# One Gram block moved into the first Gram group on two projection banks, three groups shifted, and some weights at another offset in their slots

## The chip, the core and the metric

The kernel runs on one core of a Trainium2 chip. A core has a matrix engine (TensorE; PE in the profile, PEld for its weight loads), a vector engine (VectorE, DVE), an activation engine (ScalarE, ACT), a general engine (GpSimd, POOL) and a queue that issues transfers (SyncE, SP). Each engine works through its own list in order and waits on semaphores of the others. Matrix products are written into PSUM, which has eight banks of 512 float32 values in each of 128 partitions; the other engines read them from there. The metric is device microseconds of one launch, a median over runs.

## What is computed

One layer of a hybrid trunk on 528 tokens (16 meta tokens and 512 inputs) of width 2048: an RMS norm, one input projection, an RWKV-7 branch of 16 heads of 64, a gated short convolution, one output projection, and a last RMS norm. Cut to what matters here:

```python
P = rmsnorm(h_res) @ w_in                     # columns: r, k, v, g of 1024 each, 128 low-rank, 4 x 1024 for the convolution
Pr = Pr + (prev - Pr) * mu_shift              # token shift
decay = exp(-exp(w_raw)); a = sigmoid(a0 + al @ a_lora_up)
kk = k * k_k / norm(k * k_k)                  # per head
for each token:                               # per head, state S of 64 x 64
    S = S * decay - (S @ kk) (kk * a)^T + v k^T
    y = S @ r
y_a = (groupnorm(y) + bonus) * silu(g_r)
y_b = Bg * conv3(Cg * hc) * silu(g_c)
out = rmsnorm(h_res + concat(y_a, y_b) @ w_out)[16:]
```

The recurrence is done in nine chunks: chunk 0 holds the meta tokens, chunks 1 to 8 hold 64 tokens each. For each pair of heads (0 to 7 in the code) and each chunk, products between the decayed keys, removal vectors and queries of the chunk are needed: the Gram blocks.

## The kernel before

**Projection.** 65 column tiles of 128 are projected one after another. Operands are split into a high and a low part (`xh`, `xl` for the normalised input, `hi`, `lo` for the weights), and a product is three matmuls: hi with xh, hi with xl, lo with xh (`steps`). A tile of type k, v or low-rank takes all 528 tokens in two ranges of 256 and 272 columns; r, g, C and h take ranges of 256 and 258; B and gc take one range of 512. A tile (`main`) walks through four quarters of the contraction, in each first one range and then the other. For k the second range comes first. Each range has a PSUM bank from the pool `pm` (four banks, tag "main"), so that two tiles of two ranges fit: while one is computed, the other is read out (`scaled`, the rows named `pr_...`, `u`, `hh`, `b`, `gc` in the profile).

**Weights.** A quarter tile of weights arrives in a `raw` buffer (rows `wr`), ACT casts it to `hi`, and DVE or POOL makes `lo` (rows `w`, lines 134 and 135). Six slots of 1152 values hold them. `column` says at which value in its slot a tile's weights begin: 0, 16 or 80. In the built program the slots and the rows of `xh` and `xl` begin at the same place modulo 512 bytes, so these three columns are distances of 0, 64 and 320 bytes (320 is 192 below 512) between the weights and the input that is multiplied with them.

**Order of the work.** PE's list is written by the program itself. `fill(ns)` emits projection steps, counted at 0.43 ns for each column, until the given time is used up; between two fills the smaller work of the recurrence is emitted. The lists of DVE, ACT, POOL and SP come from a scheduler, in which `ahead()` gives some instructions a priority. Some transfers are queued by `later(ns, ...)` on the same count. Transfers of weights and of intermediate results stand in one list on SP.

**Around the change.** `prepare(i)` makes one head pair's operands: two low-rank products (`tz`, `ta`, lines 571 and 572), the tiles `bk` and `ar`, and the split squares `sq` and products `rk`. Then, before the change: a fill; a first Gram group for chunks 0 to 7 (line 681, 32 matmul records of 64 rows by 128 columns, into two banks of the pool `pz`, tag "tz", and two of `pi`, tags "misc" and "ser"); four masked copies to `gt` (line 691); a fill of 5500; a second group with chunk 8's two products, into two new "tz" tiles, one of which holds half of the norms `n2` as well; the norms (lines 713 and 714) and the bonus sums `zb`; and two more masked copies. After that `gt` goes to memory and back for a triangular solve (rows `nd`, `y`, `prod`, `tt` on DVE). The tiles `hh` and `cv` belong to the convolution.

Later stages, a recurrence over chunks (from 631 us on, among the last projection tiles) and the output projection (line 1243), are not touched.

Of the kernel before, what the change touches and what calls it, by code (L numbers as in the profile page):

```python
# [9 lines left out]
F32 = mybir.dt.float32  # L10
# [8 lines left out]
P = 128  # L19
# [6 lines left out]
NCH = SEQ // CH + 1  # L26
LP = NCH * CH
# [15 lines left out]
FW = dict(  # L43
    evac=34, start=1062, lora=2200, gram=8000, gram_b=13500, gram2=5500, misc=2000, v=2000, vt=1000, solve=24500, solve_first=30000,
    tr=3200, lev=3000, cp=4200, out=1500, begin=19500, p=2900, u=2900, s=5200, last=3700, mix=2600,
)
# [31 lines left out]
def hymba_kernel(ctx: ExitStack, tc: tile.TileContext, xt, xtok, front, w_in, w_out, pv, lup, cst, msk, gf, out):  # L78
# [35 lines left out]

    def column(j):
        what = plan[j][0]
        return {"B": 0, "gc": 0, "v": 80, "g": 80, "h": 80}.get(what, 16)
    stream += [w_out[0, g] for g in range(3)]
    quarters, chain, low = {}, {}, {}
    state = {"next": 0}  # L120
# [17 lines left out]
    def prefetch(upto):  # L138
        while state["next"] < min(upto, len(stream) if chain else N_IN):
            j = state["next"]  # L140
            raw = chain[j - N_IN] if j >= N_IN else wp.tile([P, 1024], F32, tag="raw", name=f"wr{j}", bufs=3)
            state["dma"] = nc.sync.dma_start(raw, stream[j]).ins
            with tc.high_priority(offset=WEIGHTS):
                for q in range(2):
                    split_w(2 * j + q, raw[:, q * 512 : (q + 1) * 512], nc.gpsimd if q and 10 < j < N_IN else nc.vector)
            state["next"] = j + 1
# [19 lines left out]
    pm = ph1.enter_context(tc.tile_pool(name="pm", bufs=4, space=PSUM))  # L166
    pz = ph1.enter_context(tc.tile_pool(name="pz", bufs=2, space=PSUM))
    pi = ph1.enter_context(tc.tile_pool(name="pi", bufs=1, space=PSUM))
# [150 lines left out]
    def steps(ps, ranges, k4, q, ks=range(4), rs_=range(2)):  # L319
        hi, lo = quarters[q]  # L320
        for r, (a, b) in enumerate(ranges):
            if r not in rs_:
                continue
            for k in ks:
                kt = 4 * k4 + k
                w = slice(k * P, (k + 1) * P)
                for n, (ww, xx) in enumerate(((hi, xh), (hi, xl), (lo, xh))):
                    nc.tensor.matmul(  # L328
                        ps[r], ww[:, w], xx[:, kt, a:b], start=(kt == 0 and n == 0), stop=(kt == KT - 1 and n == 2)
                    )  # L330
                    yield (b - a) * 0.43

    def banks(ranges, name, pool, tag):
        return [pool.tile([P, b - a], F32, tag=tag, name=f"ps_{name}_{r}") for r, (a, b) in enumerate(ranges)]

    def main(j, ranges, name):
        prefetch(2 * j + 4)
        ps = banks(ranges, name, pm, "main")
        for k4 in range(4):
            if k4 == 1:  # L340
                prefetch(2 * j + 5)
            for r in (1, 0) if name[0] == "k" else range(len(ranges)):
                yield from steps(ps, ranges, k4, 4 * j + k4, rs_=(r,))
        return ps

# [196 lines left out]
    def step():  # L542
        t = next(flow, None)
        if t is None:
            run_pending(float("inf"))
        else:
            clock[0] += t
            run_pending(clock[0])
        return t

    def fill(ns):
        while ns > 0:
            seen = len(ready)
            t = step()
            if t is None:
                return
            ns -= t
            if len(ready) > seen:
                ns += FW["evac"]
# [5 lines left out]
    def low_rank(i, j, up, w0, name, pad):  # L565
        t = tr(name)
        nc.gpsimd.memset(t[:, META:CH], pad)
        hi, lo = up
        for a, b in ((0, 272), (272, L)):
            z = pz.tile([P, b - a], F32, tag="tz", name=f"{name}_{a}")  # L570
            nc.tensor.matmul(z, hi[:, j], la[:, j, a:b], start=True, stop=False)
            nc.tensor.matmul(z, lo[:, j], la[:, j, a:b], start=False, stop=True)
            with tc.high_priority(offset=AHEAD):
                if a == 0:
                    nc.scalar.activation(t[:, 0:META], z[:, 0:META], AF.Tanh, bias=w0, scale=0.5)
                    nc.scalar.activation(t[:, CH : 5 * CH], z[:, META:272], AF.Tanh, bias=w0, scale=0.5)
                else:
                    nc.scalar.activation(t[:, 5 * CH : LP], z, AF.Tanh, bias=w0, scale=0.5)
            fill(FW["lora"])
        return t  # L580
# [46 lines left out]
    def prepare(i):  # L627
        p = i % 2
        until("k", i)
        k = got["k", i]  # L630
# [6 lines left out]
        tz = low_rank(i, 0, up, hv[:, 0, i : i + 1], f"tz{i}", -1.0)  # L637
# [26 lines left out]
        r = got["r", i]  # L664
# [8 lines left out]
        nc.scalar.activation(sq, k, AF.Square, scale=col(V_KK, i))  # L673
        sqh, sql = split(sq, f"sq{i}", LP)
        rh, rl = split(r, f"rk{i}", SEQ)
        fill(FW["gram_b" if p else "gram"])

        gt = cq.tile([P, 2, NCH, P], F32, tag=f"gt{p}", name=f"gt{i}")
        def gram(z, c, c0):
            for h, hs, ho in heads:  # L680
                nc.tensor.matmul(
                    z[h][:, c - c0],
                    bk[hs, c, h : h + 2, :].rearrange("p a s -> p (a s)"),
                    ar[hs, c].rearrange("p a s -> p (a s)"),
                    start=True, stop=True,
                )

        def masked(z, c0, c1):
            with ahead():
                for h in range(2):  # L690
                    nc.vector.tensor_tensor(
                        out=gt[:, h, c0:c1],
                        in0=z[h],
                        in1=gmask[:, h].unsqueeze(1).to_broadcast([P, c1 - c0, P]),
                        op=ALU.mult,
                    )


        za = [pz.tile([P, 4, P], F32, tag="tz", name=f"g{i}_0_{h}") for h in range(2)]
        zc = [pi.tile([P, 4, P], F32, tag=("misc", "ser")[h], name=f"g{i}_4_{h}") for h in range(2)]  # L700
        for c in range(8):
            gram(za if c < 4 else zc, c, c // 4 * 4)
        masked(za, 0, 4)
        masked(zc, 4, 8)
        fill(FW["gram2"])

        ze = [pz.tile([P, P + 288 * (1 - h)], F32, tag="tz", name=f"g{i}_8_{h}") for h in range(2)]
        gram([z[:, 0:P].unsqueeze(1) for z in ze], 8, 8)
        n2 = tr(f"n2{i}")
        zn = pi.tile([2, 288], F32, tag="misc", name=f"n2_{i}")  # L710
        zs = ((zn, 0, 288), (ze[0][0:2, P : P + 288], 288, LP))
        for z, a, b in zs:
            nc.tensor.matmul(z, ones[:, P : P + 2], sqh[:, a:b], start=True, stop=False)
            nc.tensor.matmul(z, ones[:, P : P + 2], sql[:, a:b], start=False, stop=True)
# [3 lines left out]
        with ahead():  # L718
            for z, a, b in zs:
                nc.scalar.copy(n2[0:2, a:b], z)  # L720
            masked([z[:, 0:P].unsqueeze(1) for z in ze], 8, 9)
        nc.scalar.copy(r, zb)
        fill(FW["misc"])

# [90 lines left out]
        v = got["v", i]  # L815
# [547 lines left out]
    z = {}  # L1363
    for u, unit in enumerate(units):
        half, prod, g = unit
# [53 lines left out]
    with tc.manual_schedule(engines={mybir.EngineType.DVE, mybir.EngineType.Activation, mybir.EngineType.Pool}):  # L1419
# [16 lines left out]
        for part in range(2):  # L1436
# [7 lines left out]
            h = here(1, 2)[:, cols]  # L1444
# [73 lines left out]
```

## Time and profile before

| | |
|---|---|
| median of 3 runs | 1010.39 us (1008.97 to 1011.24) |
| the profiled execution | 1008.48 us |
| its span, first to last instruction | 1006.6 us |
| PE busy | 993.2 us (99%) |
| DVE / ACT / POOL busy | 683.2 / 393.0 / 288.0 us |
| granted TensorE clock, mean | 0.997 |
| first projection matmul to the last one | 4.6 to 842 us |

The span leaves 1.9 us of the profiled execution outside, and that execution is 1.9 us below the median. In the rows of the order of time, the first number is the start in microseconds from the span's start, the second the duration; matmul records overlap, so the pace of PE is the distance between two starts and not the duration. An idle time in square brackets names what ended it. In rows of waits, "<-" names who was waited for.

### The profile page before, as it was taken

Reading aid. Unit: us, or ns where it says so; the run is one execution under the profiler, and the core shown is the slowest. Engines: PE = TensorE matmul, PEld = TensorE weight load, DVE = VectorE, ACT = ScalarE, POOL = GpSimd, SP = SyncE. Lnnn points to the kernel's source line nnn. Section 1 sums busy time; section 2 is a strip of 40 time slices with the busy share of each in tenths; the row PEclk is TensorE's granted clock in tenths of the full one; section 3 lists DMA queues with packets and bytes.
Section 4 is the critical chain, followed back from the end, with each engine's and each line's share of the span. In section 5 each row is a group of like instructions: output and inputs, shape, how many; then the busy total and the mean of one; then the engine's idle time right before and its main releaser. Section 6 shows DMA issues by size and latency. Waiting matters only on the chain.

```text
span 1006.6 us, 23759 instructions
## 1 busy us (share of the span) xinstructions
PE 993.2 (99%) x9723; PEld 912.7 (91%) x9723; DVE 683.2 (68%) x1305; ACT 393.0 (39%) x729; POOL 288.0 (29%) x294
## 2 busy tenths in 40 slices
PE   9999999999999999999999999999999999999996
PEld 8999998999998999998999998889888898888775
DVE  7686955587765668654668654244555697999787
ACT  7553423344313434322434322222222336546453
POOL 0123313224223423232323222223332333047001
PEclk9999999999999999999999999999999999999998
DMA  9526476446674363854273856977673688796754
GB/s 338 155 70 154 115 205 159 125 125 146 155 186 146 94 171 99 218 152 119 85 175 94 222 141 192 340 237 234 216 216 95 177 271 235 210 281 146 173 130 168
DMA packets 185181, 175.35 MB, mean 174 GB/s; under 512 B 121584, under 2 KB 142832, under 8 KB 184560
## 3 DMA queue, kind: packets, MB, share of 16 engines
q1 hardware_dynamic: 182480, 164.92, 56.9%
q0 software_dynamic: 2304, 8.39, 4.9%
q8 instruction: 76, 1.25, 0.5%
q10 hardware_dynamic: 288, 0.52, 0.1%
q14 instruction: 33, 0.27, 0.1%
HBM read 137.44 MB, written 36.35 MB: 173 GB/s over the span
## 4 chain that ended last, share of the span: by engine, by line
PE 62%; DVE 5%; DMA 2%; issue 2%; ACT 0%; POOL 0%; DVEq 0%; ACTq 0%; POOLq 0%
PE ps_gc L328 8%; PE ps_B L328 7%; PE ps_h L328 7%; PE ps_C L328 7%; PE ps_k L328 5%; PE ps_v L328 5%; PE M L1243 5%; PE ps_g L328 5%; PE ps_r L328 5%; DVE o L1216 2%; PE P L1243 2%; DMA wo<-in_w_out_dram 2%; PE Q L1243 1%; PE zy L1010 1%; PE zs L1006 1%
## 5 line engine op out<-in xcount | busy, mean ns | idle before, releaser
L135 POOL TENSOR_TENSOR w<-wr,w 128x512 fp32r<-128x512 f32 x119 | 166.8, 1403 | 365.8 <-ACT w L134 317.5
L134 ACT CAST w<-wr 128x512 fp32r<-128x512 f32 x252 | 152.9, 618 | 280.9 <-PE ps_k L328 45.2
L135 DVE TENSOR_TENSOR w<-wr,w 128x512 fp32r<-128x512 f32 x133 | 95.9, 728 | 103.6 <-ACT w L134 93.3
L328 PE MATMUL ps_k<-xh,w 128*128 128x256 f32 (+1 forms) x512 | 95.7, 284 | 0.1
L328 PE MATMUL ps_r<-xh,w 128*128 128x256 f32 (+1 forms) x512 | 95.1, 281 | 0.0
L328 PE MATMUL ps_v<-xh,w 128*128 128x272 f32 (+1 forms) x512 | 95.0, 283 | 0.0
L328 PE MATMUL ps_h<-xh,w 128*128 128x258 f32 (+1 forms) x512 | 94.0, 282 | 0.0
L328 PE MATMUL ps_C<-xh,w 128*128 128x258 f32 (+1 forms) x512 | 93.2, 281 | 0.0
L328 PE MATMUL ps_g<-xh,w 128*128 128x258 f32 (+1 forms) x512 | 91.9, 281 | 0.0
L328 PE MATMUL ps_B<-xh,w 128*128 128x512 f32 x256 | 83.4, 395 | 0.1
L328 PE MATMUL ps_gc<-xh,w 128*128 128x512 f32 x256 | 81.7, 393 | 0.3 <-DVE w L135 0.3
L328 PEld LDWEIGHTS ps_h<-xh,w 128*128 128x128 f32 x512 | 79.7, 189 | 2.3 <-issue 1.6
L328 PEld LDWEIGHTS ps_k<-xh,w 128*128 128x128 f32 x512 | 80.3, 189 | 0.7 <-DVE w L135 0.3
L328 PEld LDWEIGHTS ps_r<-xh,w 128*128 128x128 f32 x512 | 80.3, 189 | 0.2
L328 PEld LDWEIGHTS ps_v<-xh,w 128*128 128x128 f32 x512 | 80.0, 189 | 0.3
L328 PEld LDWEIGHTS ps_C<-xh,w 128*128 128x128 f32 x512 | 79.6, 189 | 0.6
L328 PEld LDWEIGHTS ps_g<-xh,w 128*128 128x128 f32 x512 | 79.3, 189 | 0.4
L328 PE MATMUL ps_k<-xl,w 128*128 128x272 f32 (+1 forms) x256 | 72.9, 285 | 0.0
L328 PE MATMUL ps_v<-xl,w 128*128 128x256 f32 (+1 forms) x256 | 72.5, 283 | 0.0
L328 PE MATMUL ps_r<-xl,w 128*128 128x256 f32 (+1 forms) x256 | 72.4, 283 | 0.0
L328 PE MATMUL ps_g<-xl,w 128*128 128x256 f32 (+1 forms) x256 | 72.3, 282 | 0.0
L328 PE MATMUL ps_C<-xl,w 128*128 128x256 f32 (+1 forms) x256 | 71.9, 281 | 0.0
(320 smaller groups left out, 2288.2 us busy)
## 6 DMA issues: line engine op xcount, KB each, us to landing
wr<-in_w_in_dram SPq DMA_DIRECT2D x126, 512.0 KB
ct<-opd SPq DMA_DIRECT2D x64, 288.0 KB
wo<-in_w_out_dram SPq DMA_DIRECT2D x25, 512.0 KB
x<-in_w_out_dram POOLq DMA_DIRECT2D x16, 512.0 KB, 5.7
opd<-ar SPq DMA_DIRECT2D x8, 576.0 KB
opd<-gt SPq DMA_DIRECT2D x16, 288.0 KB
opd<-bt SPq DMA_DIRECT2D x64, 64.0 KB
x<-in_w_out_dram SPq DMA_DIRECT2D x8, 512.0 KB
```

Source lines behind the costliest of these rows:

```text
L134: nc.scalar.copy(hi, rq)
L135: low[q] = eng.tensor_tensor(out=lo, in0=rq, in1=hi.bitcast(F32), op=ALU.subtract).ins
L328: nc.tensor.matmul(ps[r], ww[:, w], xx[:, kt, a:b], start=(kt == 0 and n == 0), stop=(kt == KT - 1 and n == 2))
L1006: nc.tensor.matmul(d[hs, j], w, x[hs], start=(a == 0), stop=(a == b - 1))
L1010: nc.tensor.matmul(d[ho, j], t[hs, o : o + CH], x[hs], start=(a == 0), stop=(a == b - 1))
L1216: nc.vector.tensor_tensor(out=lo, in0=rq, in1=hi.bitcast(F32), op=ALU.subtract)
L1243: nc.tensor.matmul(bank[s], left(prod, jj, m, s), w, start=(jj == 0 and n == 0), stop=(jj == 7 and n == 2))
```

## The change

Four things are changed. Chunk 8's two products are emitted right after those of chunks 0 to 7, as part of the first Gram group, and go to two banks of the projection's pool `pm`; their masked copies follow the four others. The second half of the norms gets a tile of its own under the tag "tz". The first Gram group of pairs 0, 1 and 3 is moved by +2000, +2500 and -4000 of the fill's count, and the fill behind it gives that back, so that norms and bonus stay at their places. The weights of the low-rank tile and of k and r begin at column 80 of their slots (as those of v, g and h did), those of C stay at 16, B and gc at 0; and k walks through its ranges in the order of the others.

```diff
     def column(j):
         what = plan[j][0]
-        return {"B": 0, "gc": 0, "v": 80, "g": 80, "h": 80}.get(what, 16)
+        return {"B": 0, "gc": 0, "C": 16}.get(what, 80)
...
-            for r in (1, 0) if name[0] == "k" else range(len(ranges)):
+            for r in range(len(ranges)):
...
-        fill(FW["gram_b" if p else "gram"])
+        shift = {0: 2000, 1: 2500, 3: -4000}.get(i, 0)
+        fill(FW["gram_b" if p else "gram"] + shift)
...
-        for c in range(8):
-            gram(za if c < 4 else zc, c, c // 4 * 4)
+        ze = [pm.tile([P, 1, P], F32, tag="main", name=f"g{i}_8_{h}") for h in range(2)]
+        for c in range(NCH):
+            gram((za, zc, ze)[c // 4], c, c // 4 * 4)
         masked(za, 0, 4)
         masked(zc, 4, 8)
-        fill(FW["gram2"])
-
-        ze = [pz.tile([P, P + 288 * (1 - h)], F32, tag="tz", name=f"g{i}_8_{h}") for h in range(2)]
-        gram([z[:, 0:P].unsqueeze(1) for z in ze], 8, 8)
+        masked(ze, 8, 9)
+        fill(FW["gram2"] - shift)
+
         n2 = tr(f"n2{i}")
-        zn = pi.tile([2, 288], F32, tag="misc", name=f"n2_{i}")
-        zs = ((zn, 0, 288), (ze[0][0:2, P : P + 288], 288, LP))
+        zn = [pool.tile([2, 288], F32, tag=t, name=f"n2_{i}_{t}") for pool, t in ((pi, "misc"), (pz, "tz"))]
+        zs = ((zn[0], 0, 288), (zn[1], 288, LP))
...
-            masked([z[:, 0:P].unsqueeze(1) for z in ze], 8, 9)
```

On PE the two groups of pair 2 stand as follows before the change (`g2_4`, `g2_8`: Gram products of chunks 4 to 7 and of chunk 8; `ps_k3`, `ps_r3`: projection tiles; `n2_2`: norms). First the end of the first group, then, some 40 rows on, the second group:

```order
L681 MATMUL g2_4_0_2908<-ar2_2643,bk2_2644 128x128
L681 MATMUL g2_4_1_2909<-ar2_2643,bk2_2644 128x128
L328 MATMUL ps_k3_0_2827<-xh_110,w66_2632 128x256 x2
...
L328 MATMUL ps_r3_1_2979<-xh_110,w68_2682 128x258 x2
L681 MATMUL g2_8_0_3002<-ar2_2643,bk2_2644 128x128
L681 MATMUL g2_8_1_3003<-ar2_2643,bk2_2644 128x128
L713 MATMUL n2_2_3007<-sq2_h_2796,ones_114 2x288
```

And after it:

```order
L682 MATMUL g2_4_0_2910<-ar2_2645,bk2_2646 128x128
L682 MATMUL g2_4_1_2911<-ar2_2645,bk2_2646 128x128
L682 MATMUL g2_8_0_2912<-ar2_2645,bk2_2646 128x128
L682 MATMUL g2_8_1_2913<-ar2_2645,bk2_2646 128x128
L328 MATMUL ps_k3_1_2830<-xh_110,w66_2634 128x272 x2
...
L328 MATMUL ps_r3_1_2987<-xh_110,w68_2684 128x258 x2
L714 MATMUL n2_2_misc_3011<-sq2_h_2798,ones_114 2x288
```

Chunk 8's products now share the first group's entry and exit, and the second group begins with the norms. The banks that `g2_8` takes were those of tile v2, and the next tile, r3, takes them next.

On DVE around pair 3's Gram group, before the change (`pr_v3`: read-out of tile v3; `prod2`, `tt2`, `y2`: the solve of pair 2; `gt3`: masked copies):

```order
L352 TENSOR_TENSOR pr_v3_3355<-ps_v3_0_3190,rs_112 128x256
L780 TENSOR_REDUCE tt2_3064<-prod2_3063 72x64
L352 TENSOR_TENSOR pr_v3_3355<-ps_v3_1_3191,rs_112 128x256
L783 TENSOR_TENSOR prod2_3063<-y2_3059,tt2_3064 72x512
L352 TENSOR_TENSOR pr_v3_3355<-ps_v3_1_3191,rs_112 128x2
L789 TENSOR_REDUCE y2_3059<-prod2_3063 72x8x8
L352 TENSOR_TENSOR pr_v3_3355<-ps_v3_1_3191,rs_112 128x14
...
L352 TENSOR_TENSOR pr_g2_3512<-ps_g2_0_3373,rs_112 128x256
L135 TENSOR_TENSOR w82_3367<-wr41_3365,w82_3367 128x512
L691 TENSOR_TENSOR gt3_3481<-g3_0_0_3482,cs_119 128x512
```

And after it:

```order
L352 TENSOR_TENSOR pr_v3_3358<-ps_v3_0_3193,rs_112 128x256
L352 TENSOR_TENSOR pr_v3_3358<-ps_v3_1_3194,rs_112 128x256
L352 TENSOR_TENSOR pr_v3_3358<-ps_v3_1_3194,rs_112 128x2
L352 TENSOR_TENSOR pr_v3_3358<-ps_v3_1_3194,rs_112 128x14
...
L135 TENSOR_TENSOR w82_3370<-wr41_3368,w82_3370 128x512
L692 TENSOR_TENSOR gt3_3447<-g3_0_0_3448,cs_119 128x512
L692 TENSOR_TENSOR gt3_3447<-g3_0_1_3449,cs_119 128x512
L692 TENSOR_TENSOR gt3_3447<-g3_4_0_3450,cs_119 128x512
L692 TENSOR_TENSOR gt3_3447<-g3_8_0_3452,cs_119 128x128
```

The last three pieces of pair 2's solve have moved ahead of the read-out of v3, whose banks chunk 8's products of pair 3 take, and the first copy of chunk 8 stands fourth among the masked copies.

On DVE at tile h0 of the convolution, before the change (`hh0`: its read-out; `cv0`: the convolution; `w50`: weights of the next tile, gc0):

```order
L352 TENSOR_TENSOR hh0_2122<-ps_h0_0_2003,rs_112 128x256
L780 TENSOR_REDUCE tt1_1848<-prod1_1847 72x64
L783 TENSOR_TENSOR prod1_1847<-y1_1843,tt1_1848 72x512
L352 TENSOR_TENSOR hh0_2122<-ps_h0_1_2004,rs_112 128x256
L789 TENSOR_REDUCE y1_1843<-prod1_1847 72x8x8
L352 TENSOR_TENSOR hh0_2122<-ps_h0_1_2004,rs_112 128x2
L429 TENSOR_SCALAR cv0_2127<-u0_1991,pvt_65,cv0_2127 128x512 x2
L135 TENSOR_TENSOR w50_1997<-wr25_1995,w50_1997 128x512
```

And after it:

```order
L789 TENSOR_REDUCE y1_1845<-prod1_1849 72x8x8
L352 TENSOR_TENSOR hh0_2124<-ps_h0_0_2005,rs_112 128x256
L352 TENSOR_TENSOR hh0_2124<-ps_h0_1_2006,rs_112 128x256
L352 TENSOR_TENSOR hh0_2124<-ps_h0_1_2006,rs_112 128x2
L429 TENSOR_SCALAR cv0_2129<-u0_1993,pvt_65,cv0_2129 128x512
L135 TENSOR_TENSOR w50_1999<-wr25_1997,w50_1999 128x512
L429 TENSOR_SCALAR cv0_2129<-u0_1993,pvt_65,cv0_2129 128x512
```

The solve of pair 1 is finished before the read-out of h0 instead of between its pieces, and the split of `w50` has moved ahead of one convolution step.

## The prediction

> **What bounds the kernel now.** I read the page first (busy time, then the chain that ended last), then PE's order of time around Gram groups and tiles, then DVE's and ACT's at the places where PE stops.
>
> ```profile
> span 1006.6 us, 23759 instructions
> PE 993.2 (99%) x9723; PEld 912.7 (91%) x9723; DVE 683.2 (68%) x1305; ACT 393.0 (39%) x729; POOL 288.0 (29%) x294
> PE 62%; DVE 5%; DMA 2%; issue 2%; ACT 0%; POOL 0%; DVEq 0%; ACTq 0%; POOLq 0%
> ```
>
> PE works 99% of the span and the other engines wait for it or for each other. A microsecond is therefore won only if PE issues its list faster or stops less; one of DVE, ACT or POOL counts only where PE ends up waiting. The change removes no matmul: the question is how closely the same ones follow each other. All 65 tiles and eight head pairs lie in this regime, so I price one pair and one tile and multiply. The sum is made against the profiled execution, 1008.48 us, which is 1.9 below the median of 1010.39.
>
> **Part 1: chunk 8's products join the first Gram group.** PE around pair 2's two groups, starts and durations:
>
> ```profile
> 213.48 0.49 PE L681 MATMUL g<-ar,bk 64*128 64x128 f32 x4
> ...
> 215.47 0.50 PE L328 MATMUL ps_k<-xh,w 128*128 128x256 f32 x2
> ...
> 221.20 0.28 PE L328 MATMUL ps_r<-xl,w 128*128 128x258 f32 x1
> 221.32 0.41 PE L328 MATMUL ps_r<-xh,w 128*128 128x258 f32 x2
> 221.65 0.49 PE L681 MATMUL g<-ar,bk 64*128 64x128 f32 x4
> 222.07 0.29 PE L713 MATMUL n<-sq_h,ones 128*2 128x288 f32 x1
> ```
>
> The first group is 16 products (32 records): 215.47 - 213.48 = 1.99 us from its first start to the next projection start. The second is 2 products (4 records): 222.07 - 221.65 = 0.42. If a product costs p and a group has a fixed cost s at its end, 16p + s = 1.99 and 2p + s = 0.42, so p = 0.112 and s = 0.196. There is a fixed cost at the entry too: two projection matmuls are 0.12 apart (221.20 to 221.32), so the last of them starts at 221.44, and the group 0.21 after it instead of 0.12: 0.09. The second group costs 0.09 + 0.42 = 0.51; in the merged group its products cost 2p = 0.22. That saves 0.29 us for each of eight pairs: **-2.3 us**. The bounds are narrow, because the removed group stands in the trace eight times with the same shape: 0.25 to 0.33 each, 2.0 to 2.6 together. No other work hides it, since PE's list has no slack there.
>
> The shifts of pairs 0, 1 and 3 move a group and give the count back behind it. A group in the middle of a tile switches as often as at its edge; I cost the moves themselves at nothing, and their waits in part 4. The gt transfers and the solve begin once all copies are done. With chunk 8's copies some 5 us earlier that is sooner, and the weight transfers behind them on SP move back by a few us at most, far less than the lead at which SP asks for weights (two and a half tiles, some 28 us). Nothing.
>
> **Part 2: distance 320 instead of 64, and k's ranges.** PE at the edges of a tile h1, v5, k6 and r6, and at two of the low-rank products that r6 has inside:
>
> ```profile
> 100.06 0.29 PE L571 MATMUL ta<-la,luh 128*128 128x272 f32 x1
> ...
> 100.31 0.41 PE L328 MATMUL ps_v<-xh,w 128*128 128x272 f32 x2
> ...
> 281.88 0.28 PE L328 MATMUL ps_h<-xh,w 128*128 128x256 f32 x1
> ...
> 293.13 0.40 PE L328 MATMUL ps_B<-xh,w 128*128 128x512 f32 x1
> ...
> 382.85 0.28 PE L328 MATMUL ps_v<-xh,w 128*128 128x256 f32 x1
> ...
> 394.38 0.28 PE L328 MATMUL ps_g<-xh,w 128*128 128x256 f32 x1
> ...
> 469.40 0.29 PE L328 MATMUL ps_k<-xh,w 128*128 128x272 f32 x1
> ...
> 481.02 0.28 PE L328 MATMUL ps_r<-xh,w 128*128 128x256 f32 x1
> ...
> 493.38 0.28 PE L328 MATMUL ps_v<-xh,w 128*128 128x256 f32 x1
> ```
>
> k and v have the same columns to compute (256 and 272), r and h too (256 and 258); k and r sit at a distance of 64 bytes, v and h at 320. k6 takes 481.02 - 469.40 = 11.62 and v5 394.38 - 382.85 = 11.53: 0.09 more at 64. r6 takes 493.38 - 481.02 = 12.36, of which eight low-rank matmuls are some 0.97 (two in 100.31 - 100.06 = 0.25, the 256-wide ones a little less): 11.39 against 11.25 for h1 (293.13 - 281.88), 0.14 more. Seven clean k tiles and seven r tiles would give 0.63 and 0.98.
>
> That it is the distance is an inference. C, which also sits at 64, runs as fast as h by the starts inside its tiles, r follows k, and k alone walks its ranges backwards. So the lower end is 0 (neither the distance nor the order is the cause) and the upper 1.6; below nothing would need v and h to run slower than k and r, which these rows exclude. I take all of k's, which gets distance and order at once, and about half of r's, which gets one of them: **-1.1 us**. The single low-rank tile is inside the rounding.
>
> **Part 3: a stop at tile gc0.** PE, DVE and ACT:
>
> ```profile
> 158.71 0.62 PE L328 MATMUL ps_gc<-xh,w 128*128 128x512 f32 x2
> 159.16 0.39 PE L328 MATMUL ps_gc<-xl,w 128*128 128x512 f32 x1
> 159.82 0.73 PE L328 MATMUL ps_gc<-xh,w 128*128 128x512 f32 x2 [0.27 <-DVE w L135]
> ```
>
> ```profile
> 153.27 1.19 DVE L783 TENSOR_TENSOR prod<-y,tt 72x512 f32<-72x512 f32 x1
> ...
> 154.71 0.69 DVE L789 TENSOR_REDUCE y<-prod 72x64 f32<-72x512 f32 x1
> 155.30 0.16 DVE L352 TENSOR_TENSOR hh<-ps_h,rs 128x2 f32<-128x2 f32 x1
> ```
>
> ```profile
> 156.87 0.72 ACT L427 ACTIVATE cv<-u,pvt 128x512 f32<-128x512 f32 x1 [12.34 <-POOL u L425]
> ```
>
> 512-column matmuls start 0.23 apart (158.71 to 159.16 is two), so the one at 159.82 was due at 159.39: 0.43 lost to the split of `w50` on DVE. That split stood behind two `cv` steps, these behind ACT's `cv`, that behind POOL's `u`, and that behind the last piece of `hh0`, which came at 155.30 after two solve pieces of 1.19 and 0.69. In the new order both pieces precede the read-out, and the split passes one `cv` step. Either move is worth more than 0.43, so the stop should go whole: **-0.4**, between 0 (something else is late, such as the cast of w50) and 0.43.
>
> **Part 4: the new waits.** `g_8` occupies the two `pm` banks of the tile before the group, so it waits until that tile is read out, and the tile after next in PE's list waits until the masked copies have emptied them. Behind a waiting Gram product stands all of PE's list. First the second wait, at the pairs with the shortest way (DVE, and PE's first matmul of the tile that takes the banks):
>
> ```profile
> 216.78 2.47 DVE L691 TENSOR_TENSOR gt<-g,cs 128x512 f32<-128x512 f32 x4
> ...
> 355.09 2.48 DVE L691 TENSOR_TENSOR gt<-g,cs 128x512 f32<-128x512 f32 x4
> ```
>
> ```profile
> 218.94 0.28 PE L328 MATMUL ps_r<-xh,w 128*128 128x256 f32 x1
> ...
> 357.40 0.29 PE L328 MATMUL ps_k<-xh,w 128*128 128x272 f32 x1
> ```
>
> Four copies take 2.47, so 0.6 each from start to start; chunk 8's first stands fourth and, being a quarter as large, ends some 2.1 us after the first copy begins: 218.9 for pair 2, 357.2 for pair 4. The next tiles start at 218.94 + 0.22 = 219.16 and at 357.62. They just fit, with 0.3 and 0.4 to spare. Pairs 6 and 7 are like these, pair 5 is tighter in the first wait, pairs 0 and 1 have microseconds. I cost these at nothing; 0.3 us of DVE lateness at each of four would be 1.2.
>
> Pair 3 doesn't fit. Its group stood at 255.15 and moves 4000 of the count, some 4.2 us, to about 250.95; chunk 8's products come 1.8 later, at 252.8, and want the banks of v3. The rows of before:
>
> ```profile
> 255.15 0.49 PE L681 MATMUL g<-ar,bk 64*128 64x128 f32 x4
> ...
> 257.98 0.28 PE L328 MATMUL ps_g<-xl,w 128*128 128x256 f32 x1
> ```
>
> ```profile
> 232.27 0.49 DVE L352 TENSOR_TENSOR pr_r<-ps_r,rs 128x256 f32<-128x256 f32 x2 [0.78 <-PE ps_r L328]
> ...
> 236.95 1.36 DVE L641 TENSOR_TENSOR_SCAN cc<-smask,tz 128x576 f32<-128x576 f32 x1 [0.43 <-POOL tz L639]
> ...
> 245.47 0.76 DVE L659 TENSOR_TENSOR ta<-ta,k 128x576 f32<-128x576 f32 x1 [0.61 <-POOL ta L653]
> ...
> 251.91 0.42 DVE L352 TENSOR_TENSOR pr_v<-ps_v,rs 128x256 f32<-128x256 f32 x1
> 252.24 0.68 DVE L780 TENSOR_REDUCE tt<-prod 72x64 f32<-72x512 f32 x1
> ...
> 253.16 1.13 DVE L783 TENSOR_TENSOR prod<-y,tt 72x512 f32<-72x512 f32 x1
> ...
> 254.33 0.68 DVE L789 TENSOR_REDUCE y<-prod 72x64 f32<-72x512 f32 x1
> 254.93 0.16 DVE L352 TENSOR_TENSOR pr_v<-ps_v,rs 128x14 f32<-128x14 f32 x1
> ```
>
> The read-out of v3 ran from 251.91 to 255.09 with three solve pieces in between; now these stand ahead of it. Its four pieces together need 0.94 (3.18 less the 2.24 that the solve pieces take from start to start). If DVE has filled its earlier idle times with them (0.78 + 0.43 + 0.61 = 1.82 of the 2.24), the read-out begins at 252.33 and ends at 253.3; if none, it begins at 254.15 and ends at 255.1. Chunk 8's products would wait 0.5 to 2.3 us. A scheduled list that was rearranged mostly finds idle time, so I take a value near the low end: **+0.8**. The tile behind, g3, then starts about when it did (257.98, the row above, is its second matmul) and its banks are free at about 258.4; most of that is already in the wait.
>
> **Sum.** -2.3 - 1.1 - 0.4 + 0.8 = -3.0, of 1008.48: 1005.4 for an execution like the profiled one, and by the median **1007.3 us**. What a measurement can tell from no change is about 0.2%, 2.0 us: "same" is 1008.4 to 1012.4.
>
> **Rivals.**
>
> *The distance does nothing.* For it: C at 64 is fast. Against it: k against v, 11.62 to 11.53, with the same columns. The sum is then -2.3 - 0.4 + 0.8 = -1.9, that is 1008.5, at the edge of "same". In the Trainium skill this is what two pages come to: "SBUF — State Buffer", section "SBUF: two separate sides", has PE among the engines that never wait on anyone there, and "TensorE: Matmul & The Clock Gate", section "Back-to-back issue gap", prices a matmul by its columns alone (256 columns, 262 cycles). By them part 2 is 0; the trace disagrees about tiles with the same columns, though not about why.
>
> *The bank waits eat the gain.* Pair 3 at its upper end, 2.3, and 0.3 to 0.5 at four or five others give +3.5 to +4.3 against -3.8: 1010 to 1011. For it: margins of 0.2 to 0.4 us under a DVE that is 68% busy. Against it: the order puts chunk 8's copy fourth, before the largest rest.
>
> *Slower: the copies come late as a rule.* If at pairs 2, 4, 5, 6 and 7 DVE is engaged when the group ends, the next tile waits for whole pieces ahead of the copies (0.68 to 1.19 each): five times 1.2 and pair 3 at 2.3 are +8.3, less 3.8: 1015. It decides once the waits exceed about 5.8 us in sum. Against it: at 216.78 and 355.09 the copies of before begin as soon as the group's first bank is complete.
>
> **How the numbers follow.** Forecast 0.53, distance without effect 0.18, gain eaten 0.17, slower 0.12. The forecast's own bounds: best -2.6 - 1.6 - 0.4 + 0.5 = -4.1 (1006.3), less 1.4 for the spread of the runs below their median (1008.97 against 1010.39): 1004.9, which I widen to 1004.5 since part 2 is read from single tiles; its upper end falls in with the second case. The range 1004.5 to 1010.8 takes in the second case and most of the third. Faster: the forecast and most of the second that ends just below the edge, 0.65. Same: the rest of that and the third, 0.21. Slower: the fourth and a little of the third, 0.14.
>
> **What would show it.** One group of 36 records in about 2.2 us for each pair and none of four: part 1. k and r tiles at 11.53 and 11.25 without extras: part 2; at 11.62 and 11.39 it was not the distance. No idle time at gc0's `w50`: part 3. Idle time of PE released by DVE's `gt` or `pr_v`: part 4; more than 2 us in sum and the prediction is too low.

## The result, and the profile after

In the first comparison the changed kernel takes 1007.28 us (median of 10 runs, 1005.89 to 1009.85) against 1010.81 for the kernel before (10 runs): ratio 0.9969, interval 0.9956 to 0.9981. Two later comparisons of the same two kernels (below) give 0.9984 (0.9975 to 0.9993) and 0.9984 (0.9973 to 0.9996). The change makes the kernel faster by 1.6 to 3.1 us by these medians' ratios; the forecast was 1007.3. The first median lies on it, but in part by luck: two of the four terms behind the forecast are not right, as the traces show.

The page of the changed kernel; the profiled execution took 1008.37 us, over the median of its kernel, whereas that of the kernel before lay under its own:

```profile
span 1006.6 us, 23780 instructions
PE 992.7 (99%) x9723; PEld 913.6 (91%) x9723; DVE 688.4 (68%) x1305; ACT 392.1 (39%) x729; POOL 296.4 (29%) x294
PE 55%; DVE 9%; DMA 3%; issue 2%; ACT 1%; POOL 0%; DVEq 0%; SPq 0%; ACTq 0%; POOLq 0%
```

The two spans are equal, and yet one kernel is faster: from the first tile of v (53 us) to the first matmul of h4 (630 us) PE's starts repeat from execution to execution within 0.1 us, while the parts ahead of and behind that vary by one to three. So I compare that stretch. A view by stretches has as its columns the stretch, its length, the busy time of PE, PEld, DVE, ACT and POOL (with the number of records), the granted clock, the busy share of the transfers and their GB/s; each stretch begins and ends at a start in PE's order of time. Before the change, and after it:

```profile
53.20:630.31 577.11, 576.70 (x5505) 551.75 (x5504) 383.21 (x824) 210.15 (x387) 174.01 (x187) 1.00 0.56 147
```

```profile
54.10:628.81 574.71, 574.33 (x5506) 551.66 (x5504) 388.40 (x824) 209.71 (x387) 181.94 (x187) 1.00 0.57 147
```

2.40 us less. Where they come from, tile by tile:

*The groups.* PE around pair 2's group, after the change:

```profile
212.74 2.28 PE L682 MATMUL g<-ar,bk 64*128 64x128 f32 x36
214.95 0.52 PE L328 MATMUL ps_k<-xh,w 128*128 128x272 f32 x2
...
218.32 0.28 PE L328 MATMUL ps_k<-xh,w 128*128 128x272 f32 x1
218.45 0.28 PE L328 MATMUL ps_r<-xh,w 128*128 128x256 f32 x1
```

One group of 36 records, 214.95 - 212.74 = 2.21 us, which is 1.99 + 2 x 0.112 as reckoned. The tile r3, which takes the banks of chunk 8's products next, starts 0.13 after the matmul ahead of it: no wait. The tiles with a group are shorter by 0.26, 0.29, 0.34, 0.26, 0.30, 0.26 and 0.30 at pairs 0, 1, 2, 4, 5, 6 and 7, 2.0 together.

*Two stops gone.* Tiles gc0 and k2, before and after:

```profile
153.47:165.09 11.62, 11.35 (x50) 8.86 (x49) 5.79 (x8) 2.80 (x5) 5.91 (x4) 1.00 0.44 99
165.09:179.62 14.53, 14.46 (x226) 13.82 (x224) 9.36 (x15) 5.54 (x10) 4.29 (x4) 1.00 0.80 208
```

```profile
153.81:164.72 10.91, 10.91 (x51) 9.02 (x50) 4.15 (x6) 2.79 (x5) 5.59 (x4) 1.00 0.76 155
164.72:178.88 14.16, 14.16 (x226) 13.75 (x224) 9.29 (x13) 5.44 (x10) 4.49 (x4) 1.00 0.54 167
```

gc0 is 0.71 shorter and k2 0.37. The prediction had one stop of 0.43. The second was there to be read in the order of time of before, in k2:

```profile
171.05 0.29 PE L328 MATMUL ps_k<-xl,w 128*128 128x272 f32 x1
171.41 0.53 PE L328 MATMUL ps_k<-xh,w 128*128 128x272 f32 x2
171.77 0.29 PE L328 MATMUL ps_k<-xl,w 128*128 128x272 f32 x1
```

The first two are 0.36 apart where 0.12 is the pace. PE's row has no bracket: one record lasts 0.29, so only 0.07 of the gap is left idle between the two, too little for the view to name. The rows of the weight loads (PEld) of the same trace do name it. k2 waited for a weight split of VectorE, as gc0 did, and gc0 has a second late load, 3 us behind its stop:

```profile
162.66 0.30 PEld L328 LDWEIGHTS ps_gc<-xh,w 128*128 128x128 f32 x2 [0.25 <-POOL w L135]
...
171.40 0.30 PEld L328 LDWEIGHTS ps_k<-xh,w 128*128 128x128 f32 x2 [0.29 <-DVE w L135]
```

A stop also costs more than its gap, because the matmul behind the late one starts 0.11 late too: at k2 two matmuls take 0.36 (171.41 to 171.77) instead of 0.24, and at gc0 they take 0.56 (159.82, in the prediction's rows, to 160.38) instead of 0.45:

```profile
160.38 0.40 PE L328 MATMUL ps_gc<-xl,w 128*128 128x512 f32 x1
...
162.67 0.74 PE L328 MATMUL ps_gc<-xh,w 128*128 128x512 f32 x2
163.24 0.40 PE L328 MATMUL ps_gc<-xl,w 128*128 128x512 f32 x1
```

At 162.67 no matmul stops, but with the weight load late the next one starts 0.11 late again (0.57 for two). So gc0's 0.71 is a gap of 0.43 and twice 0.11, and k2's 0.37 a gap of 0.24 and once 0.11; the few hundredths left are spread over other matmuls.

*Pair 3.* The tiles g2 and g3, with pair 3's group in them, before and after, and PE and DVE in the changed kernel:

```profile
244.35:270.63 26.28, 26.28 (x237) 25.54 (x235) 21.37 (x42) 9.99 (x18) 6.89 (x10) 1.00 0.53 126
```

```profile
243.28:270.31 27.03, 26.73 (x237) 25.87 (x235) 20.32 (x37) 10.30 (x18) 13.01 (x9) 1.00 0.48 116
```

```profile
249.86 2.85 PE L682 MATMUL g<-ar,bk 64*128 64x128 f32 x36
252.65 0.38 PE L328 MATMUL ps_g<-xl,w 128*128 128x256 f32 x1
...
257.48 0.28 PE L328 MATMUL ps_g<-xh,w 128*128 128x258 f32 x1
257.98 0.36 PE L328 MATMUL ps_g<-xh,w 128*128 128x256 f32 x1 [0.22 <-DVE gt L692]
```

```profile
251.23 0.89 DVE L352 TENSOR_TENSOR pr_v<-ps_v,rs 128x256 f32<-128x256 f32 x4
...
254.37 1.47 DVE L135 TENSOR_TENSOR w<-wr,w 128x512 fp32r<-128x512 f32 x1
255.76 2.87 DVE L692 TENSOR_TENSOR gt<-g,cs 128x512 f32<-128x512 f32 x6
```

0.75 longer. The group takes 252.65 - 249.86 = 2.79 instead of 2.21, since chunk 8's products wait for the read-out of v3: 0.58. Then g3 starts 257.98 - 257.48 = 0.50 after the matmul ahead of it instead of 0.12, held by the masked copies: 0.38. VectorE begins these 3.1 us after the group's last product (252.65 to 255.76), behind other work of its list. Together 0.96 against the 0.75 measured, so the merged group still saves 0.21 here.

*Distance and order.* Tiles k6 and r6, before and after:

```profile
469.40:481.02 11.62, 11.62 (x97) 11.62 (x96) 4.53 (x8) 3.11 (x5) 2.57 (x2) 1.00 0.36 115
481.02:493.38 12.36, 12.36 (x107) 12.36 (x105) 6.44 (x10) 7.31 (x16) 5.09 (x5) 1.00 0.18 48
```

```profile
468.48:480.06 11.58, 11.58 (x98) 11.58 (x96) 4.40 (x6) 3.12 (x5) 2.57 (x2) 1.00 0.35 116
480.06:492.41 12.35, 12.35 (x106) 12.35 (x105) 6.54 (x12) 7.33 (x16) 5.08 (x5) 1.00 0.19 50
```

0.04 and 0.01. The 1.1 us of this term isn't there; other k tiles move by 0.03 up or 0.01 down.

The starts show where k6 and v5 differ. A tile is eight blocks of twelve matmuls (four quarters, two ranges). k6's first block of 272 columns took 1.52 us when it opened the tile and takes 1.49 now that it comes second: that is the 0.04. The blocks of 256 columns have two paces, 1.41 us (118 ns a matmul) and 1.37 (114 ns): all four of k6 are at the slower one, of v5 the last three, of h1 and the C tile ahead of it none, and so before the change as after it. That is nearly all of the other 0.05, and it doesn't follow the distance, since C lies at 64 bytes and v5 at 320.

The sum of the stretch is -2.0 (groups), -1.1 (stops) and +0.75 (pair 3 with its group), -2.35; 0.05 is left for all the rest, with distance and order in it.

*One thing that no term had.* From the last matmul to the end of the span the kernel before takes 8.17 us and the changed one 8.57. In the last 5.6 us the queues of before carry only the output (`q10`, with the same 288 packets in both kernels, is left out here):

```profile
q1 hardware_dynamic: 498, 0.89, 42.9%
```

and those of the changed kernel one load of instructions too (`q14`):

```profile
q1 hardware_dynamic: 397, 0.71, 35.2%
q14 instruction: 1, 0.01, 0.3%
```

The kernel before has a load like it earlier: one `q14` packet at 993.8 us, 12.7 us ahead of the end of its span, where the changed kernel's comes 4.8 us ahead of the end.

### The profile page after: what moved, and what is told of

It reads as the page before. It is cut to its first block, busy times and chain, and to the rows that moved or that the text cites. A ratio compares the mean times of both kernels' runs of the same rounds, so it can differ in the third digit from the quotient of the medians.

```text
span 1006.6 us, 23780 instructions
## 1 busy us (share of the span) xinstructions
PE 992.7 (99%) x9723; PEld 913.6 (91%) x9723; DVE 688.4 (68%) x1305; ACT 392.1 (39%) x729; POOL 296.4 (29%) x294
## 4 chain that ended last, share of the span: by engine, by line
PE 55%; DVE 9%; DMA 3%; issue 2%; ACT 1%; POOL 0%; DVEq 0%; SPq 0%; ACTq 0%; POOLq 0%
PE ps_gc L328 8%; PE ps_B L328 7%; PE ps_h L328 7%; PE ps_C L328 7%; PE ps_k L328 5%; PE ps_v L328 5%; PE ps_g L328 5%; PE ps_r L328 5%; DVE o L1216 4%; DMA wo<-in_w_out_dram 2%; DVE xa L1224 1%; PE zy L1010 1%; PE zs L1006 1%; PE rz L954 1%; DVE xb L1224 1%
## 5 line engine op out<-in xcount | busy, mean ns | idle before, releaser
L135 POOL TENSOR_TENSOR w<-wr,w 128x512 fp32r<-128x512 f32 x119 | 174.4, 1466 | 348.6 <-ACT w L134 300.1
L135 DVE TENSOR_TENSOR w<-wr,w 128x512 fp32r<-128x512 f32 x133 | 98.4, 745 | 105.0 <-ACT w L134 104.7
L328 PE MATMUL ps_k<-xl,w 128*128 128x256 f32 (+1 forms) x256 | 72.9, 285 | 0.0
```

Of the source, the lines that this page charges most:

```text
L135: low[q] = eng.tensor_tensor(out=lo, in0=rq, in1=hi.bitcast(F32), op=ALU.subtract).ins
L328: nc.tensor.matmul(ps[r], ww[:, w], xx[:, kt, a:b], start=(kt == 0 and n == 0), stop=(kt == KT - 1 and n == 2))
```

## The experiments

Theory 1 is the prediction's terms, theory 2 the reading above. Twelve runs in three sets, each with its own runs of the kernel before (medians 1009.82, 1009.59 and 1009.54). "Stretch" is the time from the first v tile to the first matmul of h4 in the trace; "end" the time from the last matmul to the end of the span. Ratios are to the kernel before of the same set.

| kernel | median us | ratio (interval) | stretch | end |
|---|---|---|---|---|
| before, first trace | 1010.81 | | 577.11 | 8.17 |
| before, again | 1009.66 | 1.0006 (0.9993 to 1.0020) | 577.01 | 8.12 |
| changed, first trace | 1007.28 | 0.9969 (0.9956 to 0.9981) | 574.71 | 8.57 |
| changed, again | 1008.27 | 0.9984 (0.9975 to 0.9993) | 574.70 | 8.64 |
| changed, third | 1008.01 | 0.9984 (0.9973 to 0.9996) | 574.69 | 8.56 |
| old columns and order | 1007.72 | 0.9979 (0.9967 to 0.9991) | 575.16 | 8.57 |
| two entries | 1009.85 | 1.0002 (0.9989 to 1.0016) | 577.46 | 8.61 |
| extra work | 1016.64 | 1.0073 (1.0055 to 1.0090) | 581.77 | 8.60 |
| no shifts | 1009.01 | 0.9991 (0.9981 to 1.0001) | 576.03 | 8.68 |
| pair 0 as before | 1009.56 | 0.9999 (0.9987 to 1.0010) | 576.03 | 8.15 |
| pair 1 as before | 1007.24 | 0.9977 (0.9964 to 0.9990) | 575.10 | 8.58 |
| pair 3 as before | 1006.13 | 0.9965 (0.9952 to 0.9978) | 573.97 | 8.57 |
| the same, again | 1006.58 | 0.9976 (0.9963 to 0.9989) | 573.98 | 8.59 |
| the same, six casts moved | 1008.13 | 0.9985 (0.9972 to 0.9998) | 574.94 | 8.60 |

### The kernels as they are, again

> The kernel before, for a second trace of it. Theory 2: the stretch from the first v tile to the last gc tile takes 777.9 us within 0.6 (its recurrence part varies between executions), with the two stops at gc0 (tile 11.63 us) and k2 (14.52 us) in the same places. If the 0.7 us by which every changed kernel reached its first v tile later (53.9 to 54.1 against 53.2), and the 0.4 us more behind the last matmul (8.6 against 8.2), belong to the change, they are missing here again; if they are a matter of single executions, this trace shows about 54.0 and 8.6 too.

> The changed kernel again, for a second trace of it. Theory 1 (the terms of the prediction: 2.3 from the merged groups, 1.1 from distance and order, 0.4 from one stop, less 0.8 at pair 3): 3.0 us under the kernel before. Theory 2 (as the first trace after the change reads: 2.3 from the groups, nothing from distance and order, 1.1 from the stops at gc0 and k2, less 1.0 at pair 3): 2.4 us under it. From the first tile of v to the last tile of gc both expect the starts to repeat within 0.1 us; if the 1.5 us that the first trace loses after the projections belongs to the kernel, it comes back here too, if it is a matter of single executions, it varies.

> The changed kernel a third time, to be compared with the other kernels of this set. From the first v tile to the first h4 matmul 574.7 us as twice before; the whole 1.9 us under the kernel before by the parts that repeat (2.35 in that stretch, less 0.45 behind the last matmul).

The stretch repeats within 0.1 us for before and 0.02 for the changed kernel, so differences of a tenth there count. The first v tile came at 54.23 in the second trace of before: the 0.7 us of the start was a matter of single executions. The output projection varies the same way (166 to 170 us from the last gc tile to the last matmul, over all traces, and not by kernel). The end does not vary: 8.12 and 8.17 before, 8.56 to 8.64 after. By the parts that repeat the change is worth 2.35 - 0.45 = 1.9 us, a ratio of 0.9981, which lies inside the two later intervals and at the edge of the first.

### Distance and order undone

```diff
-        return {"B": 0, "gc": 0, "C": 16}.get(what, 80)
+        return {"B": 0, "gc": 0, "v": 80, "g": 80, "h": 80}.get(what, 16)
...
-            for r in range(len(ranges)):
+            for r in (1, 0) if name[0] == "k" else range(len(ranges)):
```

> The changed kernel with the weights of k, r and the low-rank tile back at column 16 and k's ranges back in the order 1, 0; the rest as changed. Theory 1: 1.1 us longer than the changed kernel, k tiles 0.09 and r tiles 0.07 or more longer each. Theory 2: every k and r tile as long as in the changed kernel within 0.05 us, the whole within 0.5 us, unless the other order of k's read-outs brings stops of PE, which would show as idle time with a releaser.

Tiles k6 and r6 of this kernel, and g2 with g3:

```profile
468.71:480.33 11.62, 11.62 (x97) 11.62 (x96) 4.53 (x8) 3.12 (x5) 2.58 (x2) 1.00 0.37 115
480.33:492.69 12.36, 12.36 (x107) 12.36 (x105) 6.43 (x10) 7.31 (x16) 5.09 (x5) 1.00 0.17 47
243.12:270.50 27.38, 26.72 (x236) 25.85 (x235) 22.21 (x37) 10.20 (x18) 10.67 (x9) 1.00 0.44 109
```

k6 is 0.04 longer, r6 0.01; the stretch is 0.45 longer, of which 0.35 lies at pair 3, where the other list of VectorE makes the wait longer (27.38 against 27.03). The time is the same within the interval. Theory 2: distance and order are worth about 0.1 us in all, where theory 1 had 1.1. The edit undoes both at once, but r gets the distance alone and its tile doesn't move, so the two do not hide each other.

### Two switches, all else as changed

```diff
         for c in range(NCH):
+            if c == 8:
+                fill(100)
             gram((za, zc, ze)[c // 4], c, c // 4 * 4)
...
-        fill(FW["gram2"] - shift)
+        fill(FW["gram2"] - shift - 100)
```

> The changed kernel with one projection matmul between chunk 7's and chunk 8's Gram products, so that PE switches twice for each pair as before the change, with the same banks and copies. Both theories of the group's price: a switch costs 0.29 us, so 8 x 0.29 = 2.3 us more than the changed kernel, from the second group's four records starting about 0.09 later than a projection matmul would and the next matmuls 0.2 later. Rival (the gain came from the place of the second group, in front of the norms, and not from the number of switches): less than 0.8 us more.

PE at pair 2:

```profile
213.60 2.06 PE L682 MATMUL g<-ar,bk 64*128 64x128 f32 x32
215.59 0.39 PE L328 MATMUL ps_k<-xh,w 128*128 128x272 f32 x1
215.91 0.49 PE L682 MATMUL g<-ar,bk 64*128 64x128 f32 x4
216.33 0.39 PE L328 MATMUL ps_k<-xh,w 128*128 128x272 f32 x1
```

1.99 + 0.32 + 0.42 = 2.73 us; without the projection matmul's own 0.12 that is 2.61, against 2.21 for the merged group: 0.40 for a switch. The tiles are 0.34 to 0.39 longer at seven pairs and nothing at pair 3 (27.05 against 27.03, the wait takes it in). The stretch is 2.75 longer (of 577.46), the expectation was 2.3, and the whole gain is gone (1.0002, with the two stops still away and the end still late). It is the number of switches that costs, and not the place ahead of the norms. That a switch with one matmul in between costs 0.1 more than one among many is not explained.

### More work

```diff
         nc.tensor.matmul(zb, ones[:, 0:P], rl, start=False, stop=True)
+        for _ in range(2):
+            nc.tensor.matmul(zb, ones[:, 0:P], rh, start=True, stop=False)
+            nc.tensor.matmul(zb, ones[:, 0:P], rl, start=False, stop=True)
```

> The changed kernel with the bonus sums of each pair (two 512-column matmuls) computed three times instead of once, so PE has 4 x 0.23 = 0.92 us more work at each of eight pairs, 7.4 us in the projections; outputs the same. If a microsecond of PE in the projections reaches the end whole: 7.4 us longer than the changed kernel. Rival (the output projection is bounded by its own transfers and VectorE, and takes up part of what comes before): 5 us or less longer, with the time from the last projection matmul to the end shorter by the difference.

The tiles concerned are 0.9 longer each, 7.4 together, the stretch 7.06, and the median 8.4 us over that of the changed kernel in its set. The 0.37 between 7.4 and 7.06 is a third stop that is gone here, in the B tile behind h1, which takes 12.59 to 12.64 in every other trace, before and changed, and 12.23 in this one. In the changed kernel it reads:

```profile
298.98 0.30 PEld L328 LDWEIGHTS ps_B<-xh,w 128*128 128x128 f32 x2 [0.50 <-DVE w L135]
```

Of the 1.3 by which the median goes beyond the stretch, the trace has 1.2 between h4 and the last projection matmul, where two gc tiles are 1.6 and 1.1 longer and an h tile is 1.2 shorter than in the changed kernel. The time from the last projection matmul to the last matmul is not shorter (157 us; 155 to 160 in the other traces). The rival is out: time of PE in the projections arrives at the end whole, though the chain of the output projection is full of waits for transfers and VectorE.

### The shifts undone

```diff
-        shift = {0: 2000, 1: 2500, 3: -4000}.get(i, 0)
+        shift = 0
```

> The changed kernel with the Gram groups of pairs 0, 1 and 3 at their old counts (shift 0). Theory (waits for banks): at pair 0 chunk 8's products are asked for about 80.8, before the read-out of k1 (in the changed kernel 81.7 to 82.6), so 0.5 to 1.8 us of waiting, with VectorE's read-out as releaser; at pair 1 nothing to 0.5; at pair 3 the first wait (0.58 in the changed kernel) goes and the copies come late for g3: 0.5 to 2.5 there in place of 0.96 in all. Together 0.5 to 3 us longer than the changed kernel. Rival (the shifts were of no account for waits): within 0.3 us of it. The stops at gc0 and k2: if they went with the shift of pair 1, they are back (1.08); if with the merged group, they stay away.

PE at pairs 0 and 3:

```profile
81.92 0.49 PE L682 MATMUL g<-ar,bk 64*128 64x128 f32 x2 [0.63 <-DVE pr_k L352]
...
260.36 0.39 PE L328 MATMUL ps_g<-xh,w 128*128 128x258 f32 x1 [0.93 <-DVE gt L692]
```

The two waits come at the expected places: r1 is 1.07 longer (15.80 against 14.73), the group's last records being held by the read-out of k1. At pair 3 the first wait is gone, and inside g3 the second bank comes 1.1 late, because VectorE does two weight splits and a read-out ahead of the copies and `vs` between them; 27.23 against 27.03 in sum:

```profile
257.57 1.28 DVE L692 TENSOR_TENSOR gt<-g,cs 128x512 f32<-128x512 f32 x2
258.76 0.76 DVE L821 STREAM_TRANSPOSE vs<-v 128x576 f32<-128x576 f32 x1
259.46 1.64 DVE L692 TENSOR_TENSOR gt<-g,cs 128x512 f32<-128x512 f32 x4
```

The stretch is 1.32 longer. At pair 1 the group's tile stays as it was, and v2 behind it is 0.11 longer. The stops at gc0 and k2 stay away, so the shifts, that of pair 1 among them, did not remove them.

### Pair 1, then pair 0, in the old form

```diff
-        for c in range(NCH):
-            gram((za, zc, ze)[c // 4], c, c // 4 * 4)
+        for c in range(8):
+            gram((za, zc)[c // 4], c, c // 4 * 4)
+        if i != 1:
+            ze = [pm.tile([P, 1, P], F32, tag="main", name=f"g{i}_8_{h}") for h in range(2)]
+            gram(ze, 8, 8)
...
+        else:
+            ze = [pz.tile([P, P + 288 * (1 - h)], F32, tag="tz", name=f"g{i}_8_{h}") for h in range(2)]
+            gram([z[:, 0:P].unsqueeze(1) for z in ze], 8, 8)
```

> The changed kernel with pair 1 alone in its old form: two groups, chunk 8 in front of the norms, no shift. Theory 2a (the stops at gc0 and k2 went because pair 1's copies and so its solve come earlier): g tiles 104 to 131 us longer by 0.29, gc0 tile 11.63 instead of 10.91 and k2's 14.52 instead of 14.16: 1.4 us longer than the changed kernel. Theory 2b (they went for another reason, such as the other columns or the order of the read-outs): only 0.29 longer.

Only the 0.29 of its second group (26.28 against 25.99) and 0.11 in v2 come back; gc0 and k2 stay at 10.91 and 14.17. Theory 2a falls. The same edit for pair 0:

> The changed kernel with pair 0 alone in its old form: two groups, no shift. In this form VectorE's list has the solve of pair 1 between the pieces of h0's read-out again, and the split of w50 behind two convolution steps. Theory 2c (pair 0's earlier copies start what the scheduler lists differently, and that removed the stops): gc0's tile 11.6 us instead of 10.91 and k2's 14.5 instead of 14.16, and 0.29 more in r1: 1.3 us longer than the changed kernel. Rival (the stops went with timing alone, whatever the list): gc0 and k2 as in the changed kernel, 0.3 us longer.

```profile
159.11 0.39 PE L328 MATMUL ps_gc<-xl,w 128*128 128x512 f32 x1
159.77 0.74 PE L328 MATMUL ps_gc<-xh,w 128*128 128x512 f32 x2 [0.27 <-DVE w L135]
```

The stop is back, to the hundredth (0.66 from start to start as before the change), gc0 takes 11.57 and k2 14.54, the stretch is 1.33 longer and the time that of the kernel before (0.9999). So the stops hang on the form of pair 0's group, 75 us ahead of them, and not on its shift, since without any shift they stayed away. The way is the list that the scheduler makes of VectorE's work: in this kernel the solve of pair 1 stands between the pieces of h0's read-out again, and `w50` behind two steps of `cv`:

```profile
153.22 1.19 DVE L795 TENSOR_TENSOR prod<-y,tt 72x512 f32<-72x512 f32 x1
154.34 0.41 DVE L352 TENSOR_TENSOR hh<-ps_h,rs 128x256 f32<-128x256 f32 x1
154.67 0.67 DVE L801 TENSOR_REDUCE y<-prod 72x64 f32<-72x512 f32 x1
155.26 0.14 DVE L352 TENSOR_TENSOR hh<-ps_h,rs 128x2 f32<-128x2 f32 x1
```

Both stand so in the two traces of the kernel before too. In the eleven traces without the stops the split stands ahead of the second `cv` step, and at most the last solve piece stands between the pieces of the read-out. Which of the two matters more was not tried alone.

### Pair 3 in the old form

The same edit for pair 3, with its shift taken out.

> The changed kernel with pair 3 alone in its old form: two groups, chunk 8 in front of the norms, no shift. If the waits for banks at pair 3 are 0.96 us and a second group costs 0.29 to 0.38: the tiles g2 and g3 take 26.3 instead of 27.03, 0.6 to 0.7 us shorter than the changed kernel. Theory 1 (waits 0.8, a second group 0.29): 0.5 shorter. Rival (the time at pair 3 is not the waits but the moved group itself): no shorter.

> The changed kernel with pair 3 alone in its old form, once more, for an interval beside the changed kernel. 573.97 us in the stretch to h4 as before, 0.7 less than the changed kernel, so 0.7 under it in all and 2.6 under the kernel before by the parts that repeat. Theory 1, which counts 1.1 for the distance on top: 3.5 under the kernel before.

g2 and g3 are back at 26.28, and the stretch is 573.97 and 573.98, 0.73 under the changed kernel. The waits cost more than the merged group saves, and this version is below both kernels: 1006.13 and 1006.58 us. Its intervals overlap those of the changed kernel; it is the stretch, the same in both traces, that separates them.

### Fewer instructions on ScalarE

```diff
-        nc.scalar.copy(hi, raw)
+        (nc.gpsimd.tensor_copy if i >= 2 else nc.scalar.copy)(hi, raw)
```

The edit is made in the version with pair 3 as before, and compared with it.

> The same with six casts of the low-rank weights (pairs 2 to 7) on GpSimd instead of ScalarE, which makes ScalarE's list six instructions shorter. In every changed kernel an instruction load falls into the last 5.6 us and the span ends 8.6 us behind the last matmul; in both traces of the kernel before none does, and it ends 8.15 behind. If that load is ScalarE's (its list grew by one instruction): no load there, 8.15, 0.45 us shorter than the kernel beside it. If it is SyncE's or VectorE's: 8.6 as before. In the stretch to h4 no change within 0.2.

Both expectations failed. The load of instructions is still there, 4.8 us ahead of the end as in the others, and the end is 8.60, so the length of ScalarE's list isn't its cause. And the stretch is 0.96 longer, 0.57 of it in front of r3, which waits for pair 2's masked copies:

```profile
218.51 0.38 PE L328 MATMUL ps_r<-xh,w 128*128 128x256 f32 x1 [0.41 <-DVE gt L692]
```

The margin there was 0.3 us (part 4 of the prediction). VectorE's list differs in one place only, a low-rank weight split of 0.37 us that moved some 12 us forward, and counted from the first v tile the copies begin 0.85 later. What stays of the end: in all traces with 8.1 to 8.2 (before, twice, and pair 0 as before, whose load also comes 12.7 us ahead of the end) VectorE's list has 1606 records, in those with 8.6 it has 1603 to 1605, while SyncE's and GpSimd's numbers occur on both sides. That points to VectorE's list, but no run changed it alone.

## Why the prediction came out right, step by step

1. **Merged groups, -2.3: right in mechanism and size.** Seven pairs give 2.0 (0.26 to 0.34 each, 0.29 reckoned), the eighth 0.21 under its waits; parting the group again costs 2.75.
2. **Distance and order, -1.1: wrong.** The step that failed is "k and v have the same columns to compute ... k and r sit at a distance of 64 bytes", from which 0.09 and 0.14 of a tile were put down to the distance. With the distance taken away the tiles keep their times within 0.04. The evidence against it stood in the same part (C at 64 runs as fast as h), and the prediction took only half of r's share away for it. Of the rivals, the one that the distance does nothing was right on this term, and so were the two pages of the Trainium skill cited there, "SBUF — State Buffer" ("SBUF: two separate sides") and "TensorE: Matmul & The Clock Gate" ("Back-to-back issue gap"), as far as the address goes; that equal columns always take equal time is not what the blocks show (1.37 and 1.41 us for twelve matmuls of 256 columns). What sets a block's pace, and so makes a k tile slower than a v tile, remains open. That rival's sum, -1.9, is also what the parts below come to, but with other terms in it.
3. **The stop at gc0, -0.4: right mechanism, undersized.** Two stops went, worth 0.71 and 0.37. The term took the gap of 0.43 alone, left out the 0.11 that the next matmul loses, twice here, and didn't see the stop in k2, which carries no bracket in PE's rows.
4. **New waits, +0.8: right in place, kind and nearly in size.** 0.96, as 0.58 for the read-out of v3 and 0.38 for the copies. The first is near the best case given, 0.5: the read-out ended 2.26 after the group's start (249.86 to 252.12), where the best case had 253.3 - 250.95 = 2.35. The second was reckoned at some 0.4 (257.98 to 258.4) and then put at nearly nothing by "most of that is already in the wait"; it came in full, as VectorE did other work ahead of the copies, at the end a weight split of 1.47 us. So the term is nearly right because 0.3 had been added to the best case of the first wait. At the other pairs the margins held, 0.3 at pair 2 as reckoned (copy done at 218.13, r3 at 218.45). Against the rival that the copies come late as a rule, the prediction said that those of before begin "as soon as the group's first bank is complete"; that is not so, at pair 2 they begin 1.3 us after the whole group (215.47 to 216.78), since VectorE had other pieces to do. In the rival that the waits eat the gain, five others at 0.5 would make the upper end +4.8 and not +4.3.
5. **Left out: +0.45 at the end.** No term looked behind the last matmul.

The sum by the parts that repeat is -1.9 and not -3.0. The error of +1.1 in step 2 and of 0.45 in step 5 was partly made up by 0.65 in step 3, and the first comparison happened to lie 1.5 us lower than the two later ones. That its median met 1007.3 so closely is luck; the two later medians are 0.7 and 1.0 above it. The range held each median.

## What to carry to other kernels

Where PE fills the span, count how often it switches between kinds of matmul: a small group that can join a larger one saves its entry and exit (0.3 to 0.4 us here), and that arrives at the end whole, as long as the banks it borrows come free in time; one pair in eight lost more to the bank than it gained. Before a difference of 0.1 us between two tiles is put down to a cause, look for a third tile with the same cause and without the effect, and give it its full weight. And look for stops by the distance of starts and in the rows of the weight loads, not by PE's idle time alone: records that overlap hide most of a short stop.

## What the runs showed of the hardware that was not expected

When a weight load comes late, the matmul behind the late one loses another 0.11 us (0.56 for two where 0.45 is the pace at gc0, 0.36 where 0.24 is at k2), and this even where no matmul stops (0.57 at 162.67). The distance in memory between a matmul's weights and its other operand, 64 or 320 bytes here, changes nothing that can be seen (0.01 us of r6's 12.36, 0.04 of k6's 11.62 together with the order). And a kernel whose program is hardly different can end 0.45 us later, together with a later load of instructions: in three traces it comes 12.7 us ahead of the end and the end is 8.12 to 8.17, in eleven it comes 4.8 us ahead and the end is 8.56 to 8.68. That the one causes the other is not shown.
